# Narrow matmul steps for the queries and the last feed-forward of a streaming encoder step, other first loads and other leads

## The chip, the core and the metric

The program runs on one core of one Trainium2 chip. Its engines are TensorE (PE, with its weight loads PEld), VectorE (DVE), ScalarE (ACT), GpSimd (POOL) and SyncE (SP), which only issues transfers here. Each engine works through its own list of instructions in order and waits on semaphores. The metric is the device time of one execution in microseconds, as the median of several runs.

## The reference, cut to what matters

A step of an encoder on 512 prompt tokens and 32 tokens of a running stream, 1024 channels, two layers. Each layer is feed-forward, token mixer, feed-forward; the mixer is a retention in layer 0 and a differential attention in layer 1, which reads one shared K and V made after layer 0.

```python
def swiglu(h, w_in, w_out):                      # 1024 -> 2 x 2816 -> 1024
    a, b = jnp.split(h @ w_in, 2, axis=-1)
    return (jax.nn.silu(a) * b) @ w_out

def diff_mixer(h, pos, k, v, k_past, v_past, w_q, ...):
    q = rotary((h @ w_q).reshape(b, s, H_B, 2, DH_B), pos)
    ...                                          # two softmaxes, their difference, times v
    return o.reshape(b, s, V_B) @ w_out

for l in range(DEPTH):
    h = modulate(x, g_norm[l, 0], ...)
    x = x + HALF * mod[2] * rms_norm(swiglu(h, w_ffn_in[l, 0], w_ffn_out[l, 0]), g_norm[l, 1])
    h = modulate(x, g_norm[l, 2], ...)
    y = retention_mixer(h, ...) if l < N_A else diff_mixer(h, ...)
    x = x + mod[5] * rms_norm(y, g_norm[l, 3])
    h = modulate(x, g_norm[l, 4], ...)
    x = x + HALF * mod[8] * rms_norm(swiglu(h, w_ffn_in[l, 1], w_ffn_out[l, 1]), g_norm[l, 5])
    if l == N_A - 1:
        k, v = shared_kv(x, ...)
```

Everything is float32.

## The kernel before

**Halves and units.** The 544 tokens are cut into half 0 (256 columns) and half 1 (288 columns). All large products are 368 units, numbered in the order of the network; each unit is 128 output channels of one weight matrix, and is worked once for each half. The numbers: first feed-forward 0 to 67, retention 68 to 131, second feed-forward 132 to 199, shared K and V 200 to 215, third feed-forward 216 to 283, queries 284 to 291, output of the attention 292 to 299, last feed-forward 300 to 367. A feed-forward is three parts; each has inner units (two for 128 inner channels, a first factor, `post_a`, and a second, `post_b`) and 8 output units (`out_stage`). The last part of the last feed-forward has inner units 348 to 359 and output units 360 to 367.

**Two parts of an operand.** To get float32 accuracy from the fast float32r form, every operand is split in a high and a low part (L945 and L946 for an inner product, L768 and L774 for a normalized input, L578 and L581 for the weights, which is ScalarE's cast and VectorE's difference). A product needs three of the four combinations. A unit has 8 steps (6 in the last part's output units), one for each 128 input channels. For half 1 (`run_unit`, L600) a step is three matmuls of 288 columns: high weights on the high part, high weights on the low part, low weights on the high part, all into one sum. For half 0, whose parts lie side by side, a step is one matmul of 512 columns (L603, high weights on both parts at once) and one of 256 (L605, low weights on the high part). The 512-column one leaves two sums beside each other in the bank, so a wide unit ends with `result`: ScalarE copies one sum out of PSUM (L618) and VectorE adds the other (L619). Then the bank is free.

**What sets the order.** The order is made ahead of the run by a list scheduler written in the kernel, `Sched`: each piece of work is a generator with a priority, an engine takes the ready piece with the lowest number, and the instructions are written out in that order. On the chip each engine then follows it strictly. The residual and the normalization (L838, L887, L890, L759, L774) have priority 1, weight conversions 1.05, the work after a unit 15 to 20, so of two pieces that are ready the residual's goes ahead of a unit's end. `plan` sets the sequence in which units are launched: a path of points (how many units half 0 has launched, how many half 1), read from the tables `BND` (stage changes) and `ATT` (around the attention). Half 0 runs ahead, so that TensorE has half 1's units to do while half 0's normalization runs, and the other way round. A launched unit takes one of 5 PSUM banks (`mainb`) and one of 4 weight buffers; it gives up the bank at the end of its `post` function. Transfers go over one queue of SyncE in the order of their priorities; `CT_P` (constants), `XB_P` (tokens of half 1) and `W_P` (first weights) set those of the start. `ROPE_LEAD` and `ADA_LEAD` say how many units ahead rope tables and the modulation's matmuls (L504) are asked for.

The lines: from L587 `run_unit`, from L616 `result`, from L631 `launch`, from L917 the output units, from L949 the feed-forward, from L1044 the rotation of queries and keys (L1056, L1060), L887 and L890 the residual, L829 to L838 the sum of squares, L721 to L732 its root and its spread over the rows, L1588 the logits of the attention, L1642 the transposes of its weights, L473 and L480 the first modulation.

## Time and profile before

| | us |
|---|---|
| Median of 3 runs | 2532.63 (2532.39 to 2533.38) |
| The profiled execution | 2533.88 |
| its span, first to last instruction | 2531.9 |
| TensorE busy | 2466.4 |
| VectorE busy | 1556.6 |
| ScalarE busy | 1184.1 |

How to read it: the profile is one execution. The time of a run is a little longer than the span between its first and its last instruction, here by 1.98 us. Matmuls overlap, so their mean durations are longer than the distance at which they start; what a step costs is read from start to start in the timeline. A number in brackets behind a row of the timeline is the time that the engine stood idle ahead of it, and what ended that. The granted clock is TensorE's, as a share of 2.4 GHz.

### The profile page before, as it was taken

The page shows a single profiled execution, that of the slowest core. Times are in us where ns is not written, and L with a number is a line of the kernel's source. Part 1 is how long each engine was busy: PE and PEld are TensorE (multiplying, and loading weights), DVE is VectorE, ACT ScalarE, POOL GpSimd, SP SyncE. Part 2 cuts the span into 40 slices and gives each one's busy share as a digit, 9 for nine tenths or more (in the row PEclk, how much of TensorE's full clock was granted, in tenths as well). Part 3 has the DMA queues.
Part 4 walks back from the last instruction along what each step waited for, and adds up shares of the span by engine and source line. Part 5 has one row for each costly group of instructions (what it writes and reads, how often), then busy time and mean ns, then how long its engine had stood idle before and what let it go on. Part 6 is the DMA issues. An engine that isn't in the chain of part 4 may idle for free.

```text
span 2531.9 us, 43008 instructions
## 1 busy us (share of the span) xinstructions
PE 2466.4 (97%) x16968; PEld 2213.0 (87%) x16968; DVE 1556.6 (61%) x2989; ACT 1184.1 (47%) x2400; POOL 62.1 (2%) x88
## 2 busy tenths in 40 slices
PE   7999999999999999999999999999999999998998
PEld 5999988788999998999997899998799877787998
DVE  6434436944534558434449956667777888768455
ACT  5333235643333356433236545545566655565434
POOL 0000000000000000000000000000000000000000
PEclk9999999999999999999999999999999999998999
DMA  7222258875222235422226765555745455454553
GB/s 292 92 85 100 92 207 308 314 286 201 80 82 91 79 115 197 145 99 86 92 80 213 249 210 175 174 178 192 268 156 162 161 162 194 163 169 137 167 167 112
DMA packets 124667, 413.33 MB, mean 163 GB/s; under 512 B 15281, under 2 KB 33841, under 8 KB 114225
## 3 DMA queue, kind: packets, MB, share of 16 engines
q1 hardware_dynamic: 124464, 410.59, 48.0%
q8 instruction: 133, 2.18, 0.3%
q14 instruction: 70, 0.57, 0.1%
HBM read 397.29 MB, written 13.24 MB: 162 GB/s over the span
## 4 chain that ended last, share of the span: by engine, by line
PE 86%; DVE 9%; ACT 2%; issue 2%; DMA 1%; POOL 0%; SPq 0%; DVEq 0%; POOLq 0%; ACTq 0%
PE ps L600 42%; PE ps L603 23%; PE ps L605 11%; DVE w L581 3%; PE ps L504 2%; DVE FA L759 1%; ACT w L578 1%; DVE r L774 1%; DVE FA L838 1%; DVE FA L1060 1%; PE ps L1649 1%; PE ps L1276 1%; PE ps L1264 1%; PE ps L1588 0%; PE ps L1642 0%
## 5 line engine op out<-in xcount | busy, mean ns | idle before, releaser
L600 PE MATMUL ps<-r,w 128*128 128x288 f32 x8640 | 1222.6, 297 | 4.7 <-DVE w L581 1.7
L600 PEld LDWEIGHTS ps<-r,w 128*128 128x128 f32 x8640 | 1161.3, 189 | 35.0 <-issue 14.4
L603 PE MATMUL ps<-r,w 128*128 128x512 f32 x2880 | 1045.2, 403 | 17.3 <-DVE r L774 7.1
L581 DVE TENSOR_TENSOR w<-FA,w 128x1024 fp32r<-128x1024 f32 (+1 forms) x569 | 679.7, 1195 | 459.7 <-ACT w L578 456.3
L578 ACT CAST w<-FA 128x1024 fp32r<-128x1024 f32 (+1 forms) x569 | 582.5, 1024 | 711.3 <-PE ps L600 510.8
L605 PE MATMUL ps<-r,w 128*128 128x256 f32 x2880 | 805.2, 280 | 2.2 <-DVE w L581 1.7
L603 PEld LDWEIGHTS ps<-r,w 128*128 128x128 f32 x2880 | 543.8, 189 | 149.1 <-issue 13.4
L605 PEld LDWEIGHTS ps<-r,w 128*128 128x128 f32 x2880 | 545.6, 189 | 3.7 <-DVE w L581 2.5
L618 ACT COPY FA<-ps 128x256 f32<-128x256 f32 x296 | 108.8, 368 | 219.5 <-PE ps L605 204.7
L619 DVE TENSOR_TENSOR FA<-ps,FA 128x256 f32<-128x256 f32 x296 | 123.1, 420 | 113.1 <-ACT FA L618 112.5
L933 DVE TENSOR_TENSOR FA<-ps,FA 128x256 f32<-128x256 f32 (+1 forms) x216 | 93.0, 434 | 86.0 <-PE ps L600 55.1
L945 ACT CAST r<-FA 128x256 fp32r<-128x256 f32 (+1 forms) x176 | 73.3, 417 | 72.7 <-DVE FA L992 40.9
L946 DVE TENSOR_TENSOR r<-FA,r 128x256 fp32r<-128x256 f32 (+1 forms) x176 | 76.7, 436 | 24.1 <-ACT r L945 23.4
L768 ACT ACTIVATE r<-FA,MOD 128x256 fp32r<-128x256 f32 (+1 forms) x168 | 63.7, 437 | 41.4 <-DVE FA L759 41.0
L838 DVE TENSOR_TENSOR FA<-FA 128x288 f32<-128x288 f32 (+1 forms) x168 | 72.9, 435 | 12.0 <-ACT FA L834 10.6
L992 DVE TENSOR_TENSOR FA<-ps,FA 128x288 f32<-128x288 f32 x44 | 20.1, 458 | 87.9 <-PE ps L600 87.9
L504 PE MATMUL ps<-FA,SC 128*32 128x512 f32 x576 | 69.5, 598 | 0.2 <-DMA FA<-in_ada 0.2
L727 POOL TENSOR_TENSOR FA<-FA,NHALF 128x2 f32<-128x2 f32 (+1 forms) x24 | 24.5, 1022 | 1717.9 <-DVE FA L725 1664.1
L759 DVE SCALAR_TENSOR_TENSOR FA<-X,DRV,ps 128x256 f32<-128x256 f32 (+1 forms) x168 | 57.9, 397 | 8.4 <-PE ps L732 8.0
L868 ACT ACTIVATE FA<-FA,DRV 128x256 f32<-128x256 f32 (+1 forms) x144 | 59.1, 442 | 2.9
L774 DVE SCALAR_TENSOR_TENSOR r<-FA,MOD,r 128x256 fp32r<-128x256 f32 (+1 forms) x168 | 58.9, 400 | 0.2 <-ACT r L768 0.2
L834 ACT ACTIVATE FA<-FA 128x256 f32<-128x256 f32 (+1 forms) x84 | 35.9, 427 | 21.3 <-DVE FA L933 20.0
(163 smaller groups left out, 1325.4 us busy)
## 6 DMA issues: line engine op xcount, KB each, us to landing
FA<-in_w_ffn_in SPq DMA_DIRECT2D x271, 512.0 KB, 3.5
FA<-in_ada SPq DMA_DIRECT2D x80, 1024.0 KB, 7.3
FA<-in_w_ffn_out SPq DMA_DIRECT2D x95, 512.0 KB, 3.5
FA<-in_w_in_a SPq DMA_DIRECT2D x60, 512.0 KB, 3.6
FA<-in_w_ffn_out SPq DMA_DIRECT2D x61, 384.0 KB, 3.1
FA<-in_w_kv SPq DMA_DIRECT2D x28, 512.0 KB, 4.4
FA<-in_w_out_a SPq DMA_DIRECT2D x22, 512.0 KB, 3.6
FA<-in_w_q_b SPq DMA_DIRECT2D x16, 512.0 KB, 3.6
```

The source lines that it names most:

```text
L504: te.matmul(PS[b][32 * g:32 * g + 32, :], lhsT=SC[:, k, :], rhs=fa(ada_buf[u, k], 512, g * 512), start=(k == 0), stop=(k == 7))
L578: yield act(n, lambda: nc.scalar.copy(hi, src))
L581: yield dve(n, lambda: nc.vector.tensor_tensor(lo, src, hi.bitcast(F32), ALU.subtract))
L600: te.matmul(PS[b][:, :n], lhsT=w[:, a, k, :], rhs=x, start=first and j == 0, stop=last and j == 2)
L603: te.matmul(PS[b][:], lhsT=w[:, 0, k, :], rhs=op.part[H][:].rearrange("p s n -> p (s n)"), start=first, stop=False)
L605: te.matmul(PS[b][:, :n], lhsT=w[:, 1, k, :], rhs=op.hi(H), start=False, stop=last)
L618: yield act(256, lambda: nc.scalar.copy(dst, PS[b][:, 256:]), pr)
L619: yield dvp(256, lambda: nc.vector.tensor_tensor(dst, PS[b][:, :256], dst, ALU.add), pr)
L759: nc.vector.scalar_tensor_tensor(fa(z, c1 - c0, o), X[:, f, c0:c1], DRV[:, gi, f, s:s + 1], PS[Rb][:, o:o + c1 - c0], ALU.mult, ALU.mult)
L774: nc.vector.scalar_tensor_tensor(op.lo(H, c0, c1), fa(z, c1 - c0, o), MOD[:, mi, f, s:s + 1], op.hi(H, c0, c1).bitcast(F32), ALU.add, ALU. ...
L838: yield dve(n, lambda: nc.vector.tensor_tensor(acc, acc, fa(t), ALU.add))
L933: nc.vector.tensor_tensor(Y[:, f, c], PS[b][:, o:o + n], Y[:, f, c], ALU.add)
```

## The change

It does these things:

- a unit is now marked wide or narrow when it is made. `NARROW` names the stages (1, 2) and (1, 1): the inner units of the last feed-forward and the queries. In those, half 0 works like half 1, by three matmuls of 256 columns for a step and no `result`. All output units stay wide in half 0, those of the last feed-forward too. The functions behind a unit ask by the bank (`two`) instead of the half whether there are two sums
- the constants are loaded behind the tokens of half 1, and those ahead of the second block of the modulation's weights; the second unit's weights have a slightly later priority
- the tables `BND` and `ATT`, `ROPE_LEAD` and `ADA_LEAD` have other numbers.

```diff
+NARROW = ((1, 2), (1, 1),)
...
-BND = {(0, 1): (7, 7, 7, 12), (0, 2): (8, 9, 10, 7), 'kv': (8, 9, 10, 8), (1, 0): (7, 0, 4, 0)}
+BND = {(0, 1): (7, 7, 9, 7), (0, 2): (8, 8, 11, 7), 'kv': (8, 9, 8, 8), (1, 0): (4, 0, 0, 2)}
...
-ATT = [(Q, -64, Q, -67), (Q, 0, Q, -40), (Q, 8, Q, -24), ...
+ATT = [(Q, -64, Q, -66), (Q, -1, Q, -40), (Q, 8, Q, -24), ...
...
 def run_unit(u, H, b):
+        wide = u.wide[H]
+        (two.add if wide else two.discard)(b)
...
-                if H:
+                if not wide:
                     for j, (a, x) in enumerate(((0, op.hi(H)), (0, op.lo(H)), (1, op.hi(H)))):
                         te.matmul(PS[b][:, :n], lhsT=w[:, a, k, :], rhs=x, start=first and j == 0,
                                   stop=last and j == 2)
...
     def add_unit(wap, ops, post, stage):
-        units.append(Unit(len(units), wap, ops, post, stage))
+        units.append(Unit(len(units), wap, ops, post, stage, sub[0] not in NARROW))
...
                 def post_b(H, b, sil=sil, sev=sev, op=gops[f - f0]):
                     n = COLS[H].stop - COLS[H].start
+                    w2 = b in two
                     src = PS[b][:, :n]
-                    if H == 0:
+                    if w2:
                         s = yield from get(n)
                         src = fa(s)
                         yield from result(b, src)
...
-ROPE_LEAD = 38
+ROPE_LEAD = 46
-CT_P = -0.5
-XB_P = 1.5
-W_P = {0: 0.5, 1: 1.5, 2: 2.5}
+CT_P = 0.7
+XB_P = 0.7
+W_P = {0: 0.5, 1: 1.7, 2: 2.5}
-ADA_LEAD = -66
+ADA_LEAD = -58
```

Further points of `ATT` have other numbers, but those don't move the path, since another point already holds it there. In the changed file the lines have moved down: L608 is L600 of before, L587 is L581, L733 is L725, L767 and L782 are L759 and L774, L846 is L838, L895 and L898 are L887 and L890, L958 is L946, L984 and L1004 are the products L971 and L990 of the two factors, L1625, L1663 and L1670 are L1604, L1642 and L1649 (logits of the attention, transposes of its weights, product with V).

What moves, first on VectorE where half 0 ends the inner units of the last feed-forward. Before, from the addition for unit 359 (L619, bank ps4) on, FA is scratch memory, X the residual stream:

```order
L619 TENSOR_TENSOR FA_111<-ps4_116,FA_111 128x256
L887 TENSOR_TENSOR FA_111<-FA_111,ps5_117 128x576 x2
L890 TENSOR_TENSOR X_63<-X_63,FA_111 128x2x288 x2
L887 TENSOR_TENSOR FA_111<-FA_111,ps5_117 128x576
L838 TENSOR_TENSOR FA_111<-FA_111 128x288
L890 TENSOR_TENSOR X_63<-X_63,FA_111 128x2x288
L838 TENSOR_TENSOR FA_111<-FA_111 128x288
L887 TENSOR_TENSOR FA_111<-FA_111,ps5_117 128x576
L838 TENSOR_TENSOR FA_111<-FA_111 128x288
L890 TENSOR_TENSOR X_63<-X_63,FA_111 128x2x288
L838 TENSOR_TENSOR FA_111<-FA_111 128x288
L990 SCALAR_TENSOR_TENSOR FA_111<-FA_111 128x256
```

Now, from the end of half 1's first sum of squares (L733) on:

```order
L733 TENSOR_SCALAR FA_111<-ps6_118 96x3
L1004 SCALAR_TENSOR_TENSOR FA_111<-ps0_112,FA_111 128x256
L587 TENSOR_TENSOR w2_109<-FA_111,w2_109 128x768
L958 TENSOR_TENSOR r0_5_78<-FA_111,r0_5_78 128x256
L895 TENSOR_TENSOR FA_111<-FA_111,ps6_118 128x576 x2
L898 TENSOR_TENSOR X_63<-X_63,FA_111 128x2x288
L587 TENSOR_TENSOR w0_107<-FA_111,w0_107 128x768
L898 TENSOR_TENSOR X_63<-X_63,FA_111 128x2x288
L846 TENSOR_TENSOR FA_111<-FA_111 128x288
L587 TENSOR_TENSOR w2_109<-FA_111,w2_109 128x768
```

The product of the two factors (L990, now L1004) and the low part of the last operand (L946, now L958) have moved ahead of half 1's residual, and conversions of output weights have moved in between its pieces. The first addition of an output unit's bank follows only after four pieces of each residual line, five of the squares and four conversions.

Second, on VectorE where half 1's queries are normalized. Before, the last pieces of the normalization and the addition that frees the bank of unit 307 (ps0):

```order
L774 SCALAR_TENSOR_TENSOR r1_8_98<-FA_111,MOD_67,r1_8_98 128x256
L774 SCALAR_TENSOR_TENSOR r1_8_98<-FA_111,MOD_67,r1_8_98 128x32
L581 TENSOR_TENSOR w0_107<-FA_111,w0_107 128x1024
L759 SCALAR_TENSOR_TENSOR FA_111<-X_63,DRV_68,ps5_117 128x256
L759 SCALAR_TENSOR_TENSOR FA_111<-X_63,DRV_68,ps5_117 128x32
L990 SCALAR_TENSOR_TENSOR FA_111<-FA_111 128x256 x2
L619 TENSOR_TENSOR FA_111<-ps0_112,FA_111 128x256
```

Now, where the same normalization begins; the product that frees the bank of unit 307 is L1004 from ps3:

```order
L733 TENSOR_SCALAR FA_111<-ps6_118 96x3
L984 SCALAR_TENSOR_TENSOR FA_111<-FA_111,ps1_113 128x256
L958 TENSOR_TENSOR r0_4_77<-FA_111,r0_4_77 128x256
L958 TENSOR_TENSOR r0_11_84<-FA_111,r0_11_84 128x256
L1004 SCALAR_TENSOR_TENSOR FA_111<-ps3_115,FA_111 128x256
L767 SCALAR_TENSOR_TENSOR FA_111<-X_63,DRV_68,ps6_118 128x256
L767 SCALAR_TENSOR_TENSOR FA_111<-X_63,DRV_68,ps6_118 128x32
```

What frees the bank of unit 307 stood behind the normalization and stands ahead of it now; the first that waits behind it is unit 308.

Third, on TensorE where half 0's attention begins: between the logits of its first head and the first transposes of their weights. Before:

```order
L1604 MATMUL ps7_119<-FA_111 128x128 x2
L1604 MATMUL ps5_117<-FA_111 128x256 x2
L600 MATMUL ps2_114<-r1_2_92,w0_107 128x288 x3
L600 MATMUL ps2_114<-r1_3_93,w0_107 128x288 x3
L600 MATMUL ps2_114<-r1_8_98,w0_107 128x288 x3
L600 MATMUL ps2_114<-r1_9_99,w0_107 128x288 x3
L600 MATMUL ps2_114<-r1_4_94,w0_107 128x288 x3
L600 MATMUL ps2_114<-r1_11_101,w0_107 128x288 x3
L600 MATMUL ps2_114<-r1_5_95,w0_107 128x288 x3
L600 MATMUL ps1_113<-r1_1_91,w2_109 128x288 x3
L1642 MATMUL ps7_119<-CT_64,FA_111 128x128
```

Now, its last part:

```order
L608 MATMUL ps2_114<-r1_9_99,w1_108 128x288 x3
L608 MATMUL ps2_114<-r1_4_94,w1_108 128x288 x3
L608 MATMUL ps2_114<-r1_11_101,w1_108 128x288 x3
L608 MATMUL ps2_114<-r1_5_95,w1_108 128x288 x3
L608 MATMUL ps3_115<-r0_10_83,w0_107 128x256 x3
L608 MATMUL ps3_115<-r0_12_85,w0_107 128x256 x3
L608 MATMUL ps3_115<-r0_13_86,w0_107 128x256 x3
L608 MATMUL ps3_115<-r0_1_74,w0_107 128x256 x3
L608 MATMUL ps3_115<-r0_2_75,w0_107 128x256 x3
L1663 MATMUL ps7_119<-CT_64,FA_111 128x128
```

Two steps of half 1 stand ahead of these as well, so 11 steps, five of them narrow steps of half 0, lie between where 8 lay.

## Rows read from the trace of the kernel before

**Rows 1.** The page, first section: busy us, share and instructions of each engine.

```profile
PE 2466.4 (97%) x16968; PEld 2213.0 (87%) x16968; DVE 1556.6 (61%) x2989; ACT 1184.1 (47%) x2400; POOL 62.1 (2%) x88
```

**Rows 2.** Windows: length, busy us per engine, granted PE clock, DMA share, GB/s.

```profile
0.00:36.00 36.00, 17.35 (x269) 12.99 (x273) 19.32 (x55) 14.89 (x37) 1.76 (x6) 0.91 0.96 380
...
36.00:1745.00 1709.00, 1697.20 (x11466) 1529.25 (x11458) 955.86 (x1782) 736.40 (x1439) 26.86 (x36) 1.00 0.46 156
...
1745.00:1875.00 130.00, 123.49 (x862) 105.77 (x863) 106.38 (x246) 79.10 (x209) 9.66 (x15) 0.97 0.62 215
...
1990.00:2025.00 35.00, 32.09 (x197) 27.74 (x197) 33.18 (x79) 22.05 (x48) 0.85 (x1) 0.95 0.44 146
...
2225.00:2312.00 87.00, 75.13 (x494) 65.26 (x489) 61.93 (x122) 53.61 (x114) 4.69 (x3) 0.92 0.42 136
...
2520.00:2532.00 12.00, 0.82 (x21) 0.55 (x21) 6.04 (x10) 0.86 (x3) 0.84 (x1) 0.68 0.28 99
```

**Rows 3.** Timeline of TensorE: start us, us, what, count [idle before, releaser].

```profile
1000.07 8.32 PE L600 MATMUL ps<-r,w 128*128 128x288 f32 x60
1008.23 0.39 PE L603 MATMUL ps<-r,w 128*128 128x512 f32 x1
1008.46 0.28 PE L605 MATMUL ps<-r,w 128*128 128x256 f32 x1
1008.58 0.40 PE L603 MATMUL ps<-r,w 128*128 128x512 f32 x1
```

**Rows 4.** Groups by line and form: busy us, mean ns, idle before.

```profile
L618 ACT COPY FA<-ps 128x256 f32<-128x256 f32 x296 | 108.8, 368 | 219.5 <-PE ps L605 204.7 <-DVE FA L1068 12.8 <-issue 1.6
...
L619 DVE TENSOR_TENSOR FA<-ps,FA 128x256 f32<-128x256 f32 x296 | 123.1, 420 | 113.1 <-ACT FA L618 112.5
...
L990 DVE SCALAR_TENSOR_TENSOR FA<-ps,FA 128x288 f32<-128x288 f32 x44 | 20.0, 455 | 20.1 <-PE ps L600 20.0
...
L990 DVE SCALAR_TENSOR_TENSOR FA<-FA 128x256 f32<-128x256 f32 x44 | 18.5, 422 | 1.0
...
L581 DVE TENSOR_TENSOR w<-FA,w 128x768 fp32r<-128x768 f32 x61 | 58.0, 953 | 14.2 <-ACT w L578 14.1
...
L838 DVE TENSOR_TENSOR FA<-FA 128x288 f32<-128x288 f32 x84 | 37.9, 452 | 6.8 <-ACT FA L834 6.2
```

**Rows 5.** Timeline of VectorE and TensorE where half 0 ends the last feed-forward.

```profile
2275.35 0.42 DVE L619 TENSOR_TENSOR FA<-ps,FA 128x256 f32<-128x256 f32 x1
...
2276.70 1.42 DVE L887 TENSOR_TENSOR FA<-FA,ps 128x576 f32<-128x576 f32 x2 [0.93 <-PE ps L732]
...
2283.52 0.41 DVE L990 SCALAR_TENSOR_TENSOR FA<-FA 128x256 f32<-128x256 f32 x1
...
2285.25 0.80 PE L603 MATMUL ps<-r,w 128*128 128x512 f32 x1 [6.44 <-DVE r L946]
```

**Rows 6.** Timeline of VectorE and TensorE, start of half 1's last feed-forward.

```profile
2293.32 1.20 DVE L774 SCALAR_TENSOR_TENSOR r<-FA,MOD,r 128x256 fp32r<-128x256 f32 x4
...
2305.07 0.40 PE L600 MATMUL ps<-r,w 128*128 128x288 f32 x1 [1.07 <-ACT r L768]
...
2318.75 0.43 PE L732 MATMUL ps<-CT,FA 128*128 128x128 f32 x2
```

**Rows 7.** Timeline of VectorE and TensorE at half 1's queries.

```profile
2012.02 0.41 DVE L619 TENSOR_TENSOR FA<-ps,FA 128x256 f32<-128x256 f32 x1
...
2012.49 0.80 PE L603 MATMUL ps<-r,w 128*128 128x512 f32 x1 [2.27 <-DVE FA L619]
```

**Rows 8.** Timeline of TensorE, first transposes of half 0's attention.

```profile
1803.71 0.30 PE L1642 MATMUL ps<-CT,FA 128*128 128x128 f32 x1 [2.05 <-DVE FA L1636]
```

**Rows 9.** Timeline of the first loads' waiters.

```profile
14.08 1.79 PE L473 MATMUL ps<-FA,SC 128*32 128x128 f32 x32
...
15.40 0.44 ACT L829 ACTIVATE FA<-X 128x288 f32<-128x288 f32 x1 [2.96 <-DMA X<-in_xb]
...
21.09 0.80 PE L603 MATMUL ps<-r,w 128*128 128x512 f32 x1 [4.38 <-DVE r L774]
```

More of the change, by code (lines that the diff above doesn't have):

```diff
@@ L293, with __init__ @@
 class Unit:
-    def __init__(self, idx, wap, ops, post, stage):
+    def __init__(self, idx, wap, ops, post, stage, wide):
         self.idx = idx
+        self.wide = (wide, False)
         self.wap = wap
@@ L552, in yoco_step @@
     units = []
+    sub = [None]
+    two = set()
     loads = []
@@ L918, in out_stage @@
         st = Stage(ops)
+        was = sub[0]
+        sub[0] = was, "out"
         for f in range(8):
@@ L923, in post @@
                 Y = yevs
+                w2 = b in two
                 yield from Y.ensure(H)
-                if H == 0 and first:
+                if w2 and first:
                     yield from result(b, Y[:, f, c], 15)
@@ L931, in add @@
                         def add():
-                            for o in range(0, 512 - 256 * H, 256):
+                            for o in range(0, 512 if w2 else 256, 256):
                                 nc.vector.tensor_tensor(Y[:, f, c], PS[b][:, o:o + n], Y[:, f, c], ALU.add)
-                        yield ("DVE", (2 - H) * c_dvp(n), add, 15)
+                        yield ("DVE", (1 + w2) * c_dvp(n), add, 15)
                     put_bank(b)
@@ L938, in out_stage @@
             add_unit(wview(w, k0, len(ops), f * P), ops, post, st)
+        sub[0] = was
     def split_ops(H, src, op, pr=20):
@@ L960, in post_a @@
                     n = COLS[H].stop - COLS[H].start
+                    w2 = b in two
                     t = yield from get(n)
@@ L973, in post_a @@
                         yield act(n, lambda: nc.scalar.activation(fa(t), src, AF.Silu))
-                    if H:
+                    if w2:
+                        free(s)
+                    else:
                         put_bank(b)
-                    else:
-                        free(s)
                     S.set(sev[H])
@@ L981, in post_b @@
                     n = COLS[H].stop - COLS[H].start
+                    w2 = b in two
                     src = PS[b][:, :n]
-                    if H == 0:
+                    if w2:
                         s = yield from get(n)
@@ L992, in post_b @@
                         yield dvp(n, lambda: nc.vector.tensor_tensor(fa(t), src, fa(t), ALU.mult))
-                    if H:
+                    if w2:
+                        free(s)
+                    else:
                         put_bank(b)
-                    else:
-                        free(s)
                     yield from split_ops(H, fa(t), op)
@@ L1062, in rot @@
         yield ("DVE", 2 * c_dvp(n), sw, pr)
-        if H:
+        if w2:
+            free(s)
+        else:
             put_bank(b)
-        else:
-            free(s)
         if m < n:
@@ L1099, in post_qk @@
             def post_qk(H, b, hd=hd, h=h, nm=""):
+                w2 = b in two
                 yield from piece(h, nm)
@@ L1102, in post_qk @@
                 dst = fa(hd.v[nm])[:, COLS[H]]
-                yield from rot(H, b, ret["rope"], dst)
+                yield from rot(H, b, ret["rope"], dst, w2)
                 S.set(getattr(hd, nm)[H])
@@ L1108, in post_v @@
             def post_v(H, b, hd=hd, h=h, j=0):
+                w2 = b in two
                 yield from piece(h, "v")
@@ L1131, in post_g @@
             def post_g(H, b, hd=hd, h=h, j=0):
+                w2 = b in two
                 yield from piece(h, "g")
@@ L1403, in post_k @@
             def post_k(H, b, h=h):
+                w2 = b in two
                 yield kv["rope_ev"]
@@ L1407, in post_k @@
                 t = yield from get(n)
-                yield from rot(H, b, kv["rope"], fa(t))
+                yield from rot(H, b, kv["rope"], fa(t), w2)
                 yield dma(P * n * 4, KSC[h][:, c], fa(t))
@@ L1417, in post_v @@
             def post_v(H, b, h=h):
+                w2 = b in two
                 n = COLS[H].stop - COLS[H].start
                 t = yield from get(n)
-                if H:
+                if w2:
+                    yield from result(b, fa(t))
+                else:
                     yield act(n, lambda: nc.scalar.copy(fa(t), PS[b][:, :n]))
                     put_bank(b)
-                else:
-                    yield from result(b, fa(t))
                 yield from to_tok(H, fa(t), h)
@@ L1475, in post_q @@
                 n = COLS[H].stop - COLS[H].start
+                w2 = b in two
                 yield at["rope_ev"]
@@ L1481, in post_q @@
                 yield at["qask"][H]
-                yield from rot(H, b, at["rope"], fa(at["q"][H], n, h * n), m=256 * H)
+                yield from rot(H, b, at["rope"], fa(at["q"][H], n, h * n), w2, m=256 * H)
                 S.set(at["hd"][h][H].q)
@@ L1861, in yoco_step @@
                 mark("kv")
+                sub[0] = "kv"
                 shared_kv(hkv)
```

28 lines of the change are left out of this document (15 added, 13 removed).

## The prediction

> **What bounds the kernel now.** I read the page first, then the windows by stage, then the timeline at the places where the windows leave time over. The page says that TensorE is busy for 2466.4 of 2531.9 us [rows 1], so only some 65 us of the span can be won by taking waits away, and every matmul added is paid almost in full. The windows say where those 65 us lie [rows 2]: 18.7 us before 36 us (first loads), 11.8 us spread thinly over the 1709 us that follow, 6.5 us at the queries (1745 to 1875), 2.9 us at 1990 to 2025, 11.9 us at 2225 to 2312 (where half 0 ends the last feed-forward), and 11.2 us after 2520, the last residual. The granted clock is under 1 in the same windows: 0.97, 0.95 and 0.92, that is, part of them at 1.2 GHz instead of 2.4. So the change is decided by three short places and by the price of a matmul.
>
> **The change part by part.**
>
> *Price on TensorE.* A wide step is one 512-column and one 256-column matmul; a narrow one is three of 256. 52 units of half 0 (44 of the last feed-forward, 8 of the queries) have 8 steps each: 416 steps, 416 matmuls and weight loads more. A wide step starts 0.35 us after the one before it, and in it the next matmul starts 0.12 us after a 256-column one [rows 3], with a weight load of its own in that time. Three of these are 0.36 us, so 0.006 us a step more: 416 x 0.006 = 2.5 us. From above: 60 matmuls of 288 columns take 8.16 us [rows 3], 0.136 each; less 32 columns at 2.4 GHz (0.013) that is 0.123, three are 0.369, 0.015 a step more, 6 us. From below: nothing, if the second load of the same weights costs less than a new one. I take +2.5, because a 256-column row is nearer than a 288-column one.
>
> *VectorE and ScalarE.* Each of the 52 units loses the copy of one half of its bank (368 ns) and the addition of the two halves (420 ns) [rows 4]: 19.1 us of ScalarE and 21.8 us of VectorE, most of it between 1975 and 2275. Neither engine is the bound over a stage, so this counts only where TensorE waits for them in a row. The operations that stay now read PSUM. The rows show no surcharge for that: 455 ns for 288 columns from PSUM against 422 for 256 from SBUF [rows 4], 33 ns for 32 columns, which is what the columns alone cost at 1 ns each. The Trainium skill, "VectorE: DVE Perf Modes", section on the TRN2 errata, speaks against this part: it gives a PSUM source 120 fixed cycles where an SBUF source has 58, and by that some 68 VectorE operations would each be 65 ns dearer, an estimate of 4.4 us, so that 17.4 us instead of 21.8 would be saved. These rows don't bear it out.
>
> *End of half 0 in the last feed-forward.* In a row today: the addition for the last inner unit ends at 2275.77; its product with the other factor (L990) stands behind the residual of half 1 (L887, L890) and the squares (L838) on VectorE and runs only at 2283.52; the part that TensorE needs (L946) follows, and TensorE stands for 6.44 us until 2285.25 [rows 5], then works at half clock (0.92 over this window [rows 2]). In the changed order that product needs no copy and no addition, and stands ahead of the residual. It starts when its unit ends, about 2275.2, a weight conversion of 0.95 and the second part follow, and the operand is there at about 2276.9, when TensorE has reached it. The 6.44 us go. What is late next: with five banks, the fifth output unit takes over the bank of the first, and that is set free by an addition which now stands behind four L887, four L890, five L838 and four conversions. That is 4 x 0.71 (two L887 take 1.42 from 2276.70 on [rows 5]), as much again for L890, 5 x 0.45 and 4 x 0.95 [rows 4]: 11.7 us from 2276.7 on, plus 0.8 for the addition itself (two of some 0.42): 2289.2. TensorE has done the four units before it by about 2284.1, so it stands for some 5 us instead. After that half 1's normalization paces both versions: before, TensorE still waits for it at 2305.07 [rows 6]. In the changed order VectorE has, from 2289.2 on, the end of the squares and three more banks to add (3.8), the root and its spread (2), then half 1's eight operands, each 0.6 for L759 and 0.6 for L774 (four L774, two operands, take 1.20 [rows 6]), with three conversions and some 2 us of other work between them, 14.8: the last operand comes at about 2309.8. By then TensorE has done all of half 0 and seven of eight steps of three units of half 1, for which the weights are converted; with the rest of the last (6 steps of 0.4 and three eighth steps) these three end at about 2313.3. Before, the third of them ended at 2318.75 [rows 6]. Less 0.4 for a small reduction still to come and about 1 for a stretch at half clock that follows any such stand, that is 4 us. Of the smaller waits in this window (11.9 us idle in all [rows 2], 6.44 of them named) another 1 us should go, as VectorE has less to do ahead of them. I take -5; ends +1 (the chain on VectorE becomes longer by what was put ahead of it) and -13 (idle time and half clock of this window all gone).
>
> *Start of half 1's queries.* TensorE stands 2.27 us until 2012.49, since the bank of an inner unit of half 0 is added up only at 2012.02, behind the normalization on VectorE [rows 7]. In the changed order the product that frees this bank stands ahead of that block, and the first to wait behind it is one unit later: 8 steps, 2.9 us more work for TensorE. The stand goes, and with it part of 3.4 us at half clock. -2.3, ends 0 and -4.
>
> *Start of half 0's queries.* One unit of half 0 now stands between units of half 1, so that the transposes L1642, which waited 2.05 us [rows 8], come after 11 steps instead of 8, and one more group of modulation matmuls covers the normalization. About 1 us each, and 1 us of half clock: -3; ends +1 and -6 of the 6.5 idle.
>
> *First loads.* The constants and the second modulation block go behind half 1's tokens. The second block's matmuls run at 14.08, and half 1's tokens end ScalarE's wait at 15.40 [rows 9], on a queue that moves 380 GB/s [rows 2]. 1.15 MB moved ahead puts that block back by 3 us and the first large matmul, at 21.09 [rows 9], by about 1; in exchange half 1 is normalized early and fills later waits. All loads of the first 36 us are the same bytes on a busy queue (share 0.96 [rows 2]). 0; ends -2 and +2.
>
> *Leads at the other stages.* Half 0 runs 9 to 11 units ahead instead of 7 to 9 at two stage changes, which gives half 1's normalization more cover; rope and modulation are asked for 8 units earlier and later, under work of 2.8 us a unit. Of 11.8 us idle I take -0.5; ends -4 and +4. Four weight conversions less lie beside other work: 0.
>
> Sum: +2.5 - 5 - 2.3 - 3 + 0 - 0.5 = -8.3 us. The profiled execution took 2533.88 us, 1.98 more than its span; its span would become 2523.6, and its time 2525.6. The median shown is 1.25 below that execution, so 2532.63 - 8.3 = 2524.3 us.
>
> **The rivals.** (a) *The waits are only moved.* For it: after 2276.7 VectorE decides, in either order, and TensorE waits for half 1's operands at 2305.07. Then the -5 becomes 0, the other two halve, and with the price: +2.5 - 2.7 = about 2532.4. Against it: before, TensorE had half-clock work left when the operands came. (b) *Everything goes.* With half 1's chain early too, 11 us at the end, 4 and 6 at the queries, less the price: 18.5, that is 2514. Against it: the bank that is freed late. (c) *Slower: the third weight load isn't hidden.* Narrow steps load the same weights twice in a row; if a load then shows at 60 ns, on half 0's inner units where it has only 107 ns of columns to hide under, a step costs 0.41 us, 416 x 0.06 = 25 us, and with the gains of 10.8 the time is 2547. It decides from 0.026 us a step on (10.8 / 416). Against it: a load does hide under 256 columns in each wide step [rows 3]. (d) That the change doesn't do what it says is out: the order shows 416 matmuls more and 52 copies and additions less.
>
> **How the numbers follow.** Forecast 0.60, (a) 0.16, (b) 0.14, (c) 0.10. The range takes (a) and (b) in and leaves (c) out: 2513 to 2533. Faster by over 0.2% (5.1 us, about what a measurement of this kernel can tell from no change) is the forecast, less a twentieth for its near end, and (b): 0.71. Within 0.2%: (a) and that twentieth, 0.18. Slower: (c) and the far end of (a), 0.11.
>
> **What would show it.** The price: the narrow steps' start to start, 0.36 us. The end of half 0: no wait of TensorE for L946's successor, but one of about 5 us for an addition that frees a bank. The queries of half 1: no 2 us wait for a bank near 2010. The window after 2520 should be as before. The forecast is wrong if a narrow step is over 0.37 us, if TensorE waits over 8 us between the last inner unit of half 0 and half 1's first, or if the stages before 1745 move by over 4 us.

## The result, and the profile after

The changed kernel takes 2509.47 us (median of 4 runs, 2508.64 to 2512.49) against 2532.51 (2531.98 to 2533.38): ratio 0.9911, 95% interval 0.9894 to 0.9928. That is 23 us less where 8.3 were forecast; the direction was right, the size was not, and 2509.5 lies below the range. Measured once more beside other kernels it took 2512.42 us, ratio 0.9928 (0.9916 to 0.9941), so the change is worth 19 to 23 us; the second value, too, lies just below the range. The profiled execution took 2512.49 us with a span of 2510.7.

The page, first section, of the changed kernel (answers [rows 1]):

```profile
PE 2463.0 (98%) x17384; PEld 2232.6 (89%) x17384; DVE 1533.9 (61%) x2933; ACT 1164.0 (46%) x2344; POOL 58.1 (2%) x88
```

TensorE has 416 matmuls more and is busy 3.4 us less. Busy time hides slowness: a matmul at 1.2 GHz counts as busy for longer; in the rows at 2273.10 and 2273.74 below a wide step takes 0.64 us instead of 0.35 [rows 3]. The windows show where it went; they are laid on the same work as those of [rows 2], so the later ones begin earlier.

```profile
0.00:36.00 36.00, 19.42 (x307) 14.98 (x311) 21.73 (x61) 16.73 (x41) 1.85 (x6) 1.00 0.96 378
36.00:1732.00 1696.00, 1687.09 (x11391) 1519.35 (x11391) 941.96 (x1759) 723.49 (x1419) 26.96 (x36) 1.00 0.47 156
1732.00:1862.00 130.00, 127.09 (x957) 112.99 (x956) 107.16 (x240) 78.68 (x196) 6.96 (x12) 0.99 0.62 215
1977.50:2012.50 35.00, 35.00 (x294) 33.95 (x294) 34.53 (x81) 21.22 (x44) 0.85 (x1) 1.00 0.55 171
2209.00:2291.00 82.00, 75.92 (x568) 70.50 (x567) 58.47 (x110) 51.49 (x102) 2.29 (x3) 0.96 0.50 156
2499.00:2511.00 12.00, 0.82 (x21) 0.55 (x21) 6.04 (x10) 0.87 (x3) 0.85 (x1) 0.68 0.28 98
```

In each of the first five windows TensorE has less idle time than before: 2.1, 2.9, 3.6, 2.9 and 5.8 us less, 17.3 in all. The granted clock is higher in four of them: 1.00 for 0.91, 0.99 for 0.97, 1.00 for 0.95, 0.96 for 0.92. The last window is the same.

Timeline of TensorE: narrow steps in a row; the transposes of [rows 8]; the bank at the end of half 0 (answers [rows 5]); half 1's operands (answers [rows 6]):

```profile
1969.10 13.91 PE L608 MATMUL ps<-r,w 128*128 128x256 f32 x114
1982.93 0.36 PE L729 MATMUL ps<-ONE,FA 128*32 128x2 f32 x18
...
1803.28 0.30 PE L1663 MATMUL ps<-CT,FA 128*128 128x128 f32 x1 [2.07 <-ACT w L584]
...
2272.32 0.77 PE L611 MATMUL ps<-r,w 128*128 128x512 f32 x1 [4.55 <-DVE FA L944]
...
2273.10 0.63 PE L611 MATMUL ps<-r,w 128*128 128x512 f32 x1
...
2273.74 0.63 PE L611 MATMUL ps<-r,w 128*128 128x512 f32 x1
...
2287.96 0.93 PE L608 MATMUL ps<-r,w 128*128 128x288 f32 x5 [0.80 <-DVE r L782]
```

114 matmuls (38 steps) take 13.83 us to the next start, 0.364 us a step, against 0.35 for a wide one [rows 3]. A stand is a time in which TensorE waits with nothing to do. The one for a bank came as forecast, 4.55 us for "some 5", with the forecast's queue on VectorE in front of it (L944 is the addition that frees the bank, L895 and L898 the residual, L733 half 1's root):

```profile
2260.55 1.42 DVE L895 TENSOR_TENSOR FA<-FA,ps 128x576 f32<-128x576 f32 x2
2261.89 0.75 DVE L898 TENSOR_TENSOR X<-X,FA 128x576 f32<-128x576 f32 x1
...
2271.30 0.87 DVE L944 TENSOR_TENSOR FA<-ps,FA 128x256 f32<-128x256 f32 x2
...
2276.34 0.16 DVE L733 TENSOR_SCALAR FA<-ps 96x3 f32<-96x3 f32 x1 [0.73 <-PE ps L729]
```

**Where the 23 us came from.** From the starts of TensorE's matmuls one can add up the time over the usual pace: a step's matmul is taken to last until the next start 0.120 us (256 columns, narrow), 0.132 (288), 0.232 (512) or 0.117 (256, wide), the medians of the traces; what a start is later than that is counted, and of all other matmuls only idle time before the next. Stands, half clock and small delays are all in it. The stretches are bounded in every kernel by the starts of the same units of half 0, the last one by half 1's unit 308; their names are the times in the kernel before. In us, from one profiled execution each (the middle columns are experiments 1, 7, 2, 3 and 4 below):

| stretch | before | leads only | loads only | narrow only | old loads | old leads | changed | again |
|---|---|---|---|---|---|---|---|---|
| 0 to 395, with the time until TensorE starts | 22.3 | 20.1 | 20.5 | 23.4 | 22.7 | 21.0 | 20.2 | 21.2 |
| 395 to 1731 | 37.0 | 32.1 | 36.5 | 36.4 | 33.7 | 36.6 | 33.4 | 33.2 |
| 1731 to 1854, half 0's queries | 14.9 | 9.1 | 11.5 | 9.6 | 8.5 | 10.8 | 7.8 | 9.2 |
| 1854 to 1994 | 5.4 | 7.3 | 5.8 | 4.2 | 4.0 | 4.2 | 4.4 | 4.2 |
| 1994 to 2040, half 1's queries | 5.8 | 5.9 | 5.7 | 1.3 | 1.3 | 1.3 | 1.2 | 1.2 |
| 2040 to 2215 | 8.8 | 9.4 | 8.9 | 8.1 | 7.7 | 8.1 | 7.9 | 7.9 |
| 2215 to 2335, half 0's end | 20.3 | 25.4 | 20.0 | 10.8 | 11.5 | 11.7 | 12.6 | 12.7 |
| rest | 2.9 | 2.9 | 2.9 | 2.9 | 2.9 | 2.9 | 2.9 | 2.9 |

From before to changed 26.9 us are won; TensorE's last matmul ends 21.0 us earlier (2522.8 and 2501.8), so 5.9 us were paid for the narrow steps. That price is a remainder: whatever the account misses is in it. Only 45 of before's 105.8 us (without the start) are idle time that the trace shows as such; the rest is TensorE working slowly or starting late by less than a wait that has a row. So of the 26.9 us some 17 are idle time (the windows above) and some 10 are half clock and small delays.

### The profile page after: what moved, and what is told of

Its sections match the earlier page's. It is cut to its first block, busy times and chain, and to the rows that moved or that the text cites. A ratio compares the mean times of both kernels' runs of the same rounds, so it can differ in the third digit from the quotient of the medians.

```text
span 2510.7 us, 43732 instructions
## 1 busy us (share of the span) xinstructions
PE 2463.0 (98%) x17384; PEld 2232.6 (89%) x17384; DVE 1533.9 (61%) x2933; ACT 1164.0 (46%) x2344; POOL 58.1 (2%) x88
## 4 chain that ended last, share of the span: by engine, by line
PE 89%; DVE 7%; ACT 1%; issue 1%; DMA 1%; POOL 0%; SPq 0%; DVEq 0%; POOLq 0%; ACTq 0%
PE ps L608 48%; PE ps L611 22%; PE ps L613 11%; PE ps L507 2%; DVE w L587 2%; DVE FA L767 1%; DVE r L782 1%; PE ps L1670 1%; DVE FA L1074 1%; ACT w L584 1%; PE ps L1293 1%; PE ps L1609 1%; PE ps L1281 0%; PE ps L1663 0%; DVE FA L846 0%
## 5 line engine op out<-in xcount | busy, mean ns | idle before, releaser
L608 PE MATMUL ps<-r,w 128*128 128x288 f32 (+1 forms) x9888 | 1376.0, 295 | 3.0 <-DVE r L782 1.5
L608 PEld LDWEIGHTS ps<-r,w 128*128 128x128 f32 x9888 | 1311.1, 189 | 35.1 <-issue 15.3
L587 DVE TENSOR_TENSOR w<-FA,w 128x1024 fp32r<-128x1024 f32 (+1 forms) x565 | 674.7, 1195 | 441.9 <-ACT w L584 438.2
L611 PE MATMUL ps<-r,w 128*128 128x512 f32 x2464 | 888.1, 400 | 6.4 <-DVE FA L944 4.5
L613 PE MATMUL ps<-r,w 128*128 128x256 f32 x2464 | 687.0, 279 | 0.0
L626 ACT COPY FA<-ps 128x256 f32<-128x256 f32 x244 | 90.1, 370 | 231.9 <-PE ps L613 207.6
L627 DVE TENSOR_TENSOR FA<-ps,FA 128x256 f32<-128x256 f32 x244 | 101.9, 421 | 120.6 <-ACT FA L626 120.2
L944 DVE TENSOR_TENSOR FA<-ps,FA 128x256 f32<-128x256 f32 (+1 forms) x216 | 93.2, 434 | 84.4 <-PE ps L608 55.8
L958 DVE TENSOR_TENSOR r<-FA,r 128x256 fp32r<-128x256 f32 (+1 forms) x176 | 76.4, 437 | 22.9 <-ACT r L957 22.7
L846 DVE TENSOR_TENSOR FA<-FA 128x288 f32<-128x288 f32 (+1 forms) x168 | 72.9, 435 | 11.5 <-ACT FA L842 9.7
L1006 DVE TENSOR_TENSOR FA<-ps,FA 128x288 f32<-128x288 f32 x44 | 20.1, 458 | 90.7 <-PE ps L608 90.7
L767 DVE SCALAR_TENSOR_TENSOR FA<-X,DRV,ps 128x256 f32<-128x256 f32 (+1 forms) x168 | 58.0, 396 | 3.9 <-PE ps L740 3.7
L782 DVE SCALAR_TENSOR_TENSOR r<-FA,MOD,r 128x256 fp32r<-128x256 f32 (+1 forms) x168 | 59.2, 400 | 0.3 <-ACT r L776 0.2
```

The costliest lines, as they stand in the source:

```text
L587: yield dve(n, lambda: nc.vector.tensor_tensor(lo, src, hi.bitcast(F32), ALU.subtract))
L608: te.matmul(PS[b][:, :n], lhsT=w[:, a, k, :], rhs=x, start=first and j == 0, stop=last and j == 2)
L611: te.matmul(PS[b][:], lhsT=w[:, 0, k, :], rhs=op.part[H][:].rearrange("p s n -> p (s n)"), start=first, stop=False)
L613: te.matmul(PS[b][:, :n], lhsT=w[:, 1, k, :], rhs=op.hi(H), start=False, stop=last)
L626: yield act(256, lambda: nc.scalar.copy(dst, PS[b][:, 256:]), pr)
L627: yield dvp(256, lambda: nc.vector.tensor_tensor(dst, PS[b][:, :256], dst, ALU.add), pr)
```

## The experiments

The times are medians; the kernel before, measured beside each, took 2531.3 to 2532.0.

**1. Leads and loads alone.**

```diff
-NARROW = ((1, 2), (1, 1),)
+NARROW = ()
```

> All units are wide again as in the kernel before; the leads and the order of the first loads are those of the changed kernel. Theory (what the two traces say when the time over the usual pace is added up by place: head -2.2 us, 36 to 1745 us -4, start of half 0's queries -7, start of half 1's queries -5, end of half 0 in the last feed-forward -7.5, price of narrow steps +4.5): the leads and loads own the head and the stretch up to 1745, and half of the gain at half 0's queries, so the time is about 2532.5 - 2.2 - 4 - 3.5 = 2523, and the two stands near 2010 and 2280 are back. Rival: the leads are only a retuning for the narrow units and bring nothing alone: 2532 or more.

Measured: 2530.6 us, ratio 0.9995 (0.9987 to 1.0004). The rival holds, though not for its reason: the table shows the gains of the leads, 2.2 at the head, 4.9 up to 1731 and 5.8 at the queries, but 5.1 are lost again at half 0's end and 1.9 ahead of half 1's queries. The whole column is 5.2 us below that of before; 3.4 of these are the clock of one execution (last section), and 1.8 are left, against 0.9 measured. The wide order's stand at the end is there in full:

```profile
2281.69 0.80 PE L611 MATMUL ps<-r,w 128*128 128x512 f32 x1 [6.48 <-DVE r L958]
```

**2. Narrow units alone.** The tables BND and ATT, ROPE_LEAD, ADA_LEAD, CT_P, XB_P and W_P are those of before.

```diff
-ROPE_LEAD = 46
+ROPE_LEAD = 38
...
-ADA_LEAD = -58
+ADA_LEAD = -66
```

> The narrow units of the changed kernel with the leads and the first loads of the kernel before. Theory: price +4.5, half 1's queries -5, end of half 0 -7.5, half of the gain at half 0's queries -3.5, nothing before 1745: 2532.5 - 11.5 = 2521. Rival: without leads set for them the narrow units only move the waits: 2530 or more.

Measured: 2519.5 us, ratio 0.9953 (0.9941 to 0.9966): the theory. Half 1's queries (5.8 to 1.3) and half 0's end (20.3 to 10.8) are owned by the narrow units whatever the leads.

**3. The changed kernel with the old first loads.**

```diff
-CT_P = 0.7
-XB_P = 0.7
-W_P = {0: 0.5, 1: 1.7, 2: 2.5}
+CT_P = -0.5
+XB_P = 1.5
+W_P = {0: 0.5, 1: 1.5, 2: 2.5}
```

> The changed kernel with the first loads in the order of the kernel before. Theory: the head gives back its 2.2 us and nothing else moves: 2511.7. Rival (the prediction's term of 0): 2509.5, as what the head wins is waited for later. Second rival: the loads own the gain up to 1745 too, since half 1 starts early: 2515 or more.

Measured: 2515.8 us, ratio 0.9938 (0.9925 to 0.9952), 3.4 above the second measurement of the changed kernel and 6.3 above the first; the traces show 1.5 to 2.5 us at the head and nothing behind it. The number fits the second rival, the traces the theory; against the second measurement the intervals overlap, so more than the 2 us is not shown.

**4. The changed kernel with the old leads** (BND, ATT, ROPE_LEAD and ADA_LEAD as in experiment 2, the new loads kept).

> The changed kernel with the leads (of the stage changes, the attention, rope and modulation) of the kernel before, the new order of the first loads kept. Theory: the 4 us before 1745 and some 3.5 us at half 0's queries come back: 2517. Rival: the narrow units own the gain at the queries alone and the stages before 1745 are noise: 2510.

Measured: 2517.7 us, ratio 0.9942 (0.9929 to 0.9954): the theory, 8 us above the first measurement of the changed kernel and 5 above the second. The stretch from 395 to 1731 tells the leads apart in all eight columns: 36.4 to 37.0 with the old ones, 32.1 to 33.7 with the new.

**5. Only the feed-forward narrow, and only the queries narrow.**

```diff
-NARROW = ((1, 2), (1, 1),)
+NARROW = ((1, 2),)
```

> The changed kernel, but only the 44 inner units of half 0 in the last feed-forward are narrow; the 8 query units are wide again. Theory (added up by place from the traces of the kernel before, of the changed one and of the first four runs): the inner units of the feed-forward own the start of half 1's queries (-4.6 us), the stretch behind it (-1.5) and the end of half 0 (-12.8 against the leads-only kernel), and cost 352 steps x 0.011 = +3.9; the leads-only kernel took 2530.6, so 2515.6. Rival: the query units are worth as much, as the attention starts earlier with them: 2521.

```diff
-NARROW = ((1, 2), (1, 1),)
+NARROW = ((1, 1),)
```

> The changed kernel, but only the 8 query units of half 0 are narrow; the feed-forward is wide. Theory: start of half 0's queries -1.3 and the stretch behind it -2.9 against the leads-only kernel, price 64 x 0.011 = +0.7: 2530.6 - 3.5 = 2527, and the stands near 2000 and of over 6 us near 2280 are there. Rival: worth as much as the feed-forward's: 2521.

Measured: 2512.3 us (0.9922, 0.9908 to 0.9935) and 2530.9 us (0.9996, 0.9987 to 1.0005). The feed-forward's 44 units own the whole gain of the narrow steps, as far as it can be measured; the 8 query units bring nothing that can be, less than either theory gave them.

**6. The bank at half 0's end: additions first, or shorter.** First the additions of the last output units go ahead of the residual; then these units are narrow, which halves each addition.

```diff
+            def post(H, b, f=f, p=0.5 if last and was == (1, 2) else 15):
...
-                        yield ("DVE", (1 + w2) * c_dvp(n), add, 15)
+                        yield ("DVE", (1 + w2) * c_dvp(n), add, 15 if H else p)
```

> The changed kernel, but the eight additions of half 0's last output units are put ahead of half 1's residual and squares on VectorE. The stand of 4.55 us for the bank near 2272 goes. Theory (half 1's normalization on VectorE sets the end of this window, as in the prediction): the root comes later by what is put ahead of it, 4 additions x 0.88 and some conversions x 0.95, 4 to 8 us, and TensorE waits for half 1's operands instead; against the 2509.5 of the changed kernel 0 to +4, so 2509.5 to 2513.5. Rival (the bank sets it): the stand of 4.55 and half of the 6.8 us at half clock behind it are won: 2501.5.

```diff
-        sub[0] = was, "out"
+        sub[0] = was, "out", last
...
-NARROW = ((1, 2), (1, 1),)
+NARROW = ((1, 2), (1, 1), ((1, 2), "out", True))
```

> The changed kernel, with the 8 output units of half 0 at the end of the last feed-forward narrow too, so that each of their additions takes one operation of 0.44 us instead of two. Theory: the first addition, that stands behind the residual, frees the bank 0.4 us earlier, four of them make half 1's root some 1.5 us earlier, 48 to 64 steps cost 0.011 us each, 0.7: about -1, 2508.5. Rival: the additions lie in gaps of VectorE, which waits for the squares anyway: the price alone, 2510.2.

Measured: 2517.6 us (0.9948, 0.9936 to 0.9961) and 2511.8 us (0.9923, 0.9909 to 0.9936). With the additions first the stand for the bank is gone, and TensorE stands longer for half 1, first for its sums (L729), then for its operands:

```profile
2283.20 0.39 PE L729 MATMUL ps<-ONE,FA 128*32 128x2 f32 x16 [6.83 <-DVE FA L846]
2284.40 0.49 PE L729 MATMUL ps<-ONE,FA 128*32 128x2 f32 x18 [0.80 <-DVE FA L846]
...
2288.77 0.61 PE L608 MATMUL ps<-r,w 128*128 128x288 f32 x1 [1.94 <-ACT r L776]
```

So with the bank free TensorE next waits for half 1's normalization on VectorE, as the prediction had it. The price of delaying that, 5 us against the second measurement and 8 against the first, is above the expected 0 to 4; part of it can be clock, since 13.7 us at 1.2 GHz lie at this stand, 6.8 at that of the changed kernel. The halved additions can't be told from no change.

**7. Price, loads alone, and the clock behind a stand.** The changed kernel once more; then with half 0's units of the retention narrow too, all but its outputs (384 steps, not the 400 to 450 expected); then the kernel before with the new loads alone (experiment 3's values of CT_P, XB_P and W_P the other way round, nothing else); then the kernel before with idle matmuls in its stand of [rows 7].

> The changed kernel once more, for a comparison on one chip with the runs beside it: 2509.5, if the first measurement stands; the kernel with the old first loads took 2515.8 on another call, so about 2513 would say that these 6 us were mostly spread between runs, and that the loads are worth the 2 us that the traces show.

```diff
-NARROW = ((1, 2), (1, 1),)
+NARROW = ((1, 2), (1, 1), (0, 1))
```

> The changed kernel with half 0 of all 64 units of the second stage (queries, keys, values, gates and outputs of the first attention) narrow as well but its output units: a stage without stands of TensorE, so that the price of a narrow step shows by itself. Theory (starts of matmuls in the changed kernel's trace: 3 x 0.120 against 0.232 + 0.117): 0.011 us a step, about 400 to 450 steps more, +4.5 to +5, so 2514 to 2515. Rival (the prediction's 0.006): +2.5, 2512. Second rival (nothing, as the work taken from VectorE and ScalarE pays it back through smaller waits at the stage's 30 transposes): 2509.5.

> The kernel before with nothing changed but the order of the first loads. Theory (from the traces): the head is 2 us shorter and nothing else moves: 2530.5. Rival (the prediction's 0): 2532. Second rival: 6 us, as the comparison of the changed kernel with and without it says: 2526.

```diff
+                if u.idx == 311 and H == 0 and first:
+                    x = op.part[H][:].rearrange("p s n -> p (s n)")
+                    for _ in range(9):
+                        te.matmul(PS[miscb.free[0]][:], lhsT=x[:, :P], rhs=x, start=True, stop=True)
```

> The kernel before with nine idle matmuls of 512 columns (2 us, into a free bank that nothing reads) put ahead of the first step of the unit that waits 2.27 us for its bank near 2012. The wait is as long as before, but TensorE has work in it. Theory (a stand costs its length and, behind it, half of the time at half clock): no stretch at 1.2 GHz follows, and the units behind the stand end 1.7 us earlier, while the stand of 2.3 us stays, filled. Rival: the stretch at half clock comes from something else and stays; nothing moves.

Measured: the changed kernel took 2512.4 us, so the second reading of its expectation holds. With the retention narrow 2520.7 (0.9958, 0.9946 to 0.9971), 8.3 more. 384 steps at 0.011 to 0.014 are 4.2 to 5.4; the account over pace finds 3.3 us more between 395 and 919, in waits for VectorE at this stage's transposes. Less these, 5.0 us are left, 0.013 a step, twice the prediction's 0.006, and relief of VectorE pays none of it back. The loads alone: 2529.4 us (0.9991, 0.9982 to 1.0000), 2 us at the edge of what can be told, and 1.8 at the head by the table. The filled stand, windows and timeline:

```profile
1986.00:2021.00 35.00, 34.20 (x215) 29.37 (x215) 34.55 (x80) 22.80 (x50) 0.85 (x1) 1.00 0.50 160
```

```profile
2006.75 2.23 PE L601 MATMUL ps<-r 128*128 128x512 f32 x9
2009.17 0.50 PE L607 MATMUL ps<-r,w 128*128 128x512 f32 x1 [0.19 <-DVE FA L623]
2009.51 0.28 PE L609 MATMUL ps<-r,w 128*128 128x256 f32 x1
2009.62 0.40 PE L607 MATMUL ps<-r,w 128*128 128x512 f32 x1
```

The granted clock is 1.00 instead of 0.95 [rows 2]. The time over pace from 1994 to 2040 is 2.1 plus the 2.2 of the idle matmuls, 4.3 against 5.8: 1.5 us, close to the 1.7 that the theory named, half of 3.4 us at 1.2 GHz. The same units take 44.4 us from first start to last, 45.9 in the kernel before and 45.7 with the loads alone. The single run took 2530.5 us; 1.5 us is within the spread between runs.

**8. What was still open: does the clock count at half 0's end?** Idle matmuls in the stand of the changed kernel and in that of the kernel before; then a version with the narrow outputs of experiment 6 and two filled stands.

```diff
+                if (u.idx, H, k) == (364, 0, 0):
+                    x = u.ops[0].part[H][:].rearrange("p s n -> p (s n)")
+                    for _ in range(20):
+                        te.matmul(PS[miscb.free[0]][:], lhsT=x[:, :P], rhs=x, start=True, stop=True)
```

> The changed kernel with 20 idle matmuls of 512 columns (4.3 us, into a free bank that nothing reads) in the stand of 4.55 us for the bank near 2272; the order of all else is the same. Theory N (half 1's normalization on VectorE sets the end of this window, as the prediction had it): the 6.8 us at half clock go, but TensorE then waits longer for half 1's operands: 0 to -1 against the changed kernel (2509.5 and 2512.4 in two measurements). Theory C (the clock counts in full here too): -3.4, that is about 2508.

In the kernel before it is unit 360, step 5, with 28 matmuls.

> The kernel before with 28 idle matmuls (6.1 us) in its stand of 6.44 us near 2280, where half 0 ends the last feed-forward. Theory C (half clock behind this stand is what the prediction left out of its -5): the 13.7 us at 1.2 GHz go, and half 1's third unit comes 5 to 6.8 us earlier: 2525 to 2526.5. Theory N (half 1's normalization paces TensorE from there on): the waits for half 1's operands near 2304 grow by as much, and the time stays at 2531.

> A version meant to beat both kernels: the changed one with the last eight output units of half 0 narrow (2511.8 by itself), 18 idle matmuls in the stand near 2272 and nine of 128 columns in the stand of 2.07 us near 1803. By theory C both stretches at 1.2 GHz go, 1.7 + 1.7 to 3.4 us: 2507. By theory N only the 1.7 at 1803: 2510. Where the clock doesn't fall behind the stand near 1803 in a run anyway, that part is nothing.

Measured: 2511.2 us (0.9917, 0.9903 to 0.9930), 2532.2 us (1.0002, 0.9993 to 1.0011) and 2512.3 us (0.9919, 0.9905 to 0.9932). Windows of TensorE's work from the start of unit 359 on, for the changed kernel, for that of experiment 3 and with the stand filled, then for the kernel before and with its stand filled:

```profile
2254.00:2299.00 45.00, 38.84 (x275) 33.67 (x273) 39.92 (x90) 29.88 (x62) 1.75 (x2) 0.92 0.39 117
```

```profile
2258.40:2303.40 45.00, 38.90 (x281) 33.66 (x280) 41.53 (x94) 29.08 (x61) 2.45 (x3) 0.96 0.46 130
```

```profile
2255.00:2300.00 45.00, 43.30 (x308) 37.25 (x308) 41.83 (x95) 30.05 (x64) 2.45 (x3) 1.00 0.45 127
```

```profile
2271.00:2319.00 48.00, 37.32 (x250) 31.33 (x248) 39.16 (x92) 27.28 (x60) 4.91 (x3) 0.86 0.34 106
```

```profile
2269.00:2317.00 48.00, 42.88 (x286) 36.25 (x285) 39.99 (x94) 28.35 (x61) 4.91 (x3) 0.96 0.37 110
```

The clock came back, from 0.92 to 1.00 and from 0.86 to 0.96; the medians moved by less than they can tell. The traces tell more. From unit 359 on TensorE, VectorE and ScalarE work in the same order in the kernels of experiments 3 and 5 (feed-forward only) as in the changed one, but with other stretches at 1.2 GHz, so these executions differ in little but the clock:

| | at 1.2 GHz, us | unit 359 to TensorE's last matmul, us |
|---|---|---|
| changed | 6.8 | 246.4 |
| changed again | 6.8 | 246.4 |
| experiment 5 | 3.4 behind the stand, 3.4 later | 245.9 |
| experiment 3 | 3.4 | 245.3 |
| stand filled | 0 | 244.2 |

In the changed kernel the clock counts for 2.2 us, and the waits for half 1's operands don't grow as theory N would have it: the first is 0.72 us with the stand filled, 0.80 in the changed kernel. So the mechanism is theory C's. Of its 3.4 us 0.5 can't be won, since 1.0 of the 6.8 us lies in the stand itself; the other 0.7 are not accounted for. In the kernel before theory N's 2531 came true, but by the trace not for its reason: the same stretch becomes 1 us shorter (250.2 for 251.3, which the loads alone have too), and the wait near 2304 is 1.07 us as in [rows 6]. Where the rest of theory C's 5 to 6.8 us went is not shown in full; the waits at this place beside the stand grow by 0.8 us. First the wait for half 1's operands in the changed kernel with its stand filled, then in the kernel before with its stand filled:

```profile
2286.63 0.93 PE L612 MATMUL ps<-r,w 128*128 128x288 f32 x5 [0.72 <-DVE r L786]
```

```profile
2302.09 0.40 PE L604 MATMUL ps<-r,w 128*128 128x288 f32 x1 [1.07 <-ACT r L772]
```

The version with two fills met neither theory's 2507 or 2510. No version here is measurably faster than the changed kernel.

## Why the prediction was wrong in size

The sum's terms beside what the table finds between the two profiled executions, and where one pair can mislead, in others:

| term | forecast | found |
|---|---|---|
| price of narrow steps | +2.5 | +5.9 (by starts at full pace alone +4.6) |
| end of half 0 | -5 | -7.7 |
| start of half 1's queries | -2.3 | -4.6 |
| start of half 0's queries | -3 | -7.1 in this pair, some -3 in others |
| first loads | 0 | -2.1 |
| leads at other stages | -0.5 | -3.6 |
| 1854 to 1994 and 2040 to 2215 | not priced | -1.9 |
| sum | -8.3 | -21.1 |

**The step that failed** is how waits were turned into time. The prediction took the windows' idle time (some 65 us) as all there was to win and priced the stands with a row of their own; what had none got nothing, or a guess. Its gains came to 10.8 us, half clock included; 17.3 us of idle time went, and some 10 us of half clock and small delays besides. By place:

- *Leads, "of 11.8 us idle I take -0.5".* They gave 3.6 by the table, in all four traces with new leads and in none with old. Experiment 1 adds that by themselves they are lost again at half 0's end. The term was also read in part: by the third numbers of `BND` half 0's lead rose at two stage changes (7 to 9 and 10 to 11), but fell at two others (10 to 8 and 4 to 0).
- *Smaller waits at half 0's end, "another 1 us".* The stand itself went as forecast: 6.44 us gone, 4.55 for the bank instead. From the start of unit 360 to half 1's unit 310 the changed kernel takes 61.6 us, before 66.5: the forecast's -5, with the half clock behind the new stand at 2.2 us where the sum had about 1. But ahead of unit 360 there is some 2.7 us more, in waits such as these two of the kernel before, which the changed one hasn't got:

```profile
2232.45 0.39 PE L605 MATMUL ps<-r,w 128*128 128x256 f32 x1 [0.57 <-DVE FA L1666]
2238.41 0.39 PE L605 MATMUL ps<-r,w 128*128 128x256 f32 x1 [0.75 <-DVE w L581]
```

- *Start of half 1's queries.* The mechanism was right: in the changed kernel's window from 1977.5 on TensorE is busy for 35.00 of 35 us. The size was half. The sum took the stand of 2.27 us and, of the "3.4 us at half clock" that it named, nothing; experiment 7 puts that at 1.5. A second wait for a bank, 0.58 us at 1994, was not seen.
- *Start of half 0's queries.* The transposes were to wait 1 us less behind three more steps: they wait 2.07 us, before 2.05, so that mechanism failed. What went are the waits ahead of them, for half 1's normalization, rows of before:

```profile
1759.15 0.31 PE L721 MATMUL ps<-ONE,FA 128*32 128x2 f32 x16 [1.04 <-DVE FA L838]
...
1777.92 0.50 PE L603 MATMUL ps<-r,w 128*128 128x512 f32 x1 [0.96 <-DVE r L774]
```

  The size of 3 was about right by luck, as other waits went than the forecast's: three other executions with the order of before at this place have 11.5, 11.5 and 11.7 us over pace, not 14.9, the changed order 7.8, 9.2 and 8.5. The other 4 us are mostly that one execution's clock (last section). The difference between 23 and 19 us is another matter: 1.2 us of it are the medians of the kernel before, 2.9 those of the changed one, and no trace explains it.
- *First loads, 0.* The first large matmul of half 0 came 2.3 us later (23.40 for 21.09 [rows 9]), as the prediction had it, but half 1's first came 6.5 earlier (24.2 for 30.7), and the pair is 2 us ahead at the end of the head. The bound of -2 was the better value, as experiments 3 and 7 say too.
- *Price, +2.5.* Half of what it was, or less (the 5.9 is a remainder). The prediction's own rounded times, 0.36 and 0.35 us, differ by 0.010 us, not 0.006, which is 4.2 us. By the medians it is 0.360 against 0.349 (0.232 and 0.117), 0.011 a step, and the row with its delays has 0.364. The upper bound, 6, was the better value.

Of the rivals, (c) is out: a step takes 0.364 us, not 0.41. (a) describes the leads alone. (b), everything goes, gave 2514, the number nearest to both measurements, but by luck: the bank's stand that spoke against it is there. Of the points that would make it wrong one came true: the stages before 1745 moved by 5.7 us.

The part on PSUM came out as the rows had it. In the changed kernel the product of an inner unit reads PSUM in the 22 narrow units and SBUF in the 22 wide ones of half 0:

```profile
L1004 DVE SCALAR_TENSOR_TENSOR FA<-FA 128x256 f32<-128x256 f32 x22 | 9.4, 425 | 0.7
...
L1004 DVE SCALAR_TENSOR_TENSOR FA<-ps,FA 128x256 f32<-128x256 f32 x22 | 9.1, 421 | 3.9 <-PE ps L608 3.7
```

421 ns from PSUM, 425 from SBUF. The Trainium skill, "VectorE: DVE Perf Modes", section on the TRN2 errata, gives the PSUM source 62 more fixed cycles; these rows disagree, and the measurement decides.

## What to carry to other kernels

A share of idle time is not what can be won: add up, stretch by stretch, how much later than the usual pace TensorE's matmuls start, and price a change against that, half clock and sub-microsecond waits included. A stand costs its length plus what runs slowly behind it: by the traces 1.5 us behind the one near 2012, 2.2 behind the one near 2272, and 1 behind the one of before near 2280, where other waits come next. To find this out, compare traces of one order that differ in the clock alone, or fill the stand. Leads and orders set for one shape of the work are not a gain by themselves: here the leads were worth 5 to 8 us with the narrow units, and leads and loads together nothing that could be measured without.

## What the runs showed of the hardware

**The clock falls behind the same stand in one run and not in another.** Near 1750 to 1785 the kernel before and the same order in experiment 7's filled kernel have nearly the same waits (1.04 and 0.83, then 1.20 and 0.96 in both), with 31.31 and 31.52 us busy of 35:

```profile
1750.00:1785.00 35.00, 31.31 (x231) 26.31 (x233) 30.50 (x59) 18.65 (x36) 2.31 (x2) 0.95 0.63 214
```

```profile
1750.00:1785.00 35.00, 31.52 (x242) 25.74 (x242) 30.25 (x59) 19.27 (x36) 2.33 (x2) 1.00 0.66 216
```

The granted clock is 0.95 in the one and 1.00 in the other; the one has 3.4 us at 1.2 GHz from 1780.3 on and again from 1804.2 on behind the stand of [rows 8], the other neither. The Trainium skill, "TensorE: Matmul & The Clock Gate", Part 1, says of a kernel's start that the number of matmuls at the lower clock differs between runs of one kernel. These traces show the like in mid-kernel, as do the 6.8 and 3.4 us behind one stand in the table of experiment 8. A term for half clock, worked out from one profiled execution, is therefore uncertain by all of itself: here 3.4 us (14.9 over pace for 11.5) in a stretch of 123.

**Idle matmuls hold the clock.** Nine of 512 columns in a stand of 2.3 us kept it at 1.00, where three traces of this order without them (before, loads alone, end filled) have 3.4 to 6.8 us at 1.2 GHz; 20 in one of 4.6 us kept it at 1.00 too. 28 in the stand of 6.4 us did so in part (0.96 for 0.86). What the traces win by it, 1.0 to 2.2 us, is too little for the times to tell.
